# Factors and probabilities turned by TensorE, and all operations issued in the order of a list scheduling inside the kernel

## The chip, the cores and the metric

The kernel runs on one core of one Trainium2 chip. The metric is the device time of one launch in microseconds (us), the median of several runs. One core has five engines that run side by side, each taking its own instructions strictly in order: TensorE (PE: matmuls and transposes into the accumulators, PSUM), VectorE (DVE), ScalarE (ACT), GpSimd (POOL) and SyncE (SP), which here issues nearly all DMA transfers. They wait for one another through semaphores.

## The reference

One layer over 256 tokens of width 4096, in float32. A projection by `w_in` feeds 16 heads of softmax attention with a forget gate ("fox", head size 128), 32 heads of an RWKV-7 recurrence (head size 64) and a gate `z`; the gated results go through `w_out`, a residual and a LayerNorm.

```python
proj = jnp.einsum('bsd,dc->bsc', x, w_in)
...
logits = jnp.einsum('bhqd,bhkd->bhqk', qb, kf) + cb[..., :, None] - c[..., None, :]
logits = jnp.where(key_pos[None, :] <= q_pos[:, None], logits, -jnp.inf)
p = jax.nn.softmax(logits, axis=-1)
...
state = (state * w_t[:, :, None, :] + sa[..., None] * b_t[:, :, None, :]
         + v_t[..., None] * k_t[:, :, None, :])
return state, jnp.einsum('bhvk,bhk->bhv', state, r_t)
...
h = jnp.concatenate([fox_out, rwkv_out], axis=-1) * jax.nn.silu(z.astype(f32))
out = jnp.einsum('bsc,cd->bsd', h.astype(x.dtype), w_out)
x = _layernorm(ALPHA * x.astype(f32) + out.astype(f32), ln_gain, ln_bias, LN_EPS).astype(x.dtype)
```

## The kernel before

**The large matmuls.** x and every weight are split in two float32r halves, high (h) and low (l), and each product is three matmuls of 128x128 by 128x512: x high by w high (L146), x low by w high (L147), x high by w low (L148). Weights stream in pieces of 512 KB, `w{n}_{b}_{q}` (`w4_1_7` in the order, `w_7` in the profile, which leaves n and b out): SyncE loads one (L218), ScalarE makes the high half (`w_7h`, L140), VectorE the low one (`w_7l`, L141). A piece feeds 12 large matmuls. Buffers allow four raw pieces, four high and three low ones, and `weights` (L238) keeps up to three split pieces ready ahead. There are 8 head pairs n, each with 4 blocks b (block 0: r and k, 1: v of both kinds, 2 and 3: q, k and the gates of the fox heads 2n and 2n+1), each with 16 pieces q; then the output projection with 8 blocks of 16 pieces (`project`, L860 to L862). That makes 7680 large matmuls.

**The work between.** What the heads need besides runs as Python generators, which `slot` (L198) advances by a step after every two of the (j, m) steps; the order in which they emit is then the program's, apart from the framework's scheduler and from operations pinned by `keep_in_program_order` or `issue_after`. Numbers of slots to wait stand in the table `W` and in constants (LAG, LAND, BEHIND).

- `unload` takes a finished block: two VectorE transposes of `bk` (L789), a trip through HBM (`bt`) and back as `fq`, `fk`, `zf`, `zr` or `raw`. For the last pair TensorE turns them instead (`tr`, L815).
- `prepare` makes the factors `BK`, `lt` and the decays of one half of a pair (`np` on TensorE).
- `rwkv` (L505) computes a pair's recurrence by chunks of 64: the products `gp` (L517), which give `Nb` by a trip through HBM; the inverse of a triangular matrix on VectorE, 31 steps of a product and a sum (`prod`, L579, and `xc`, L582; called the solver below), whose result goes out as `td` and comes back as `T` (L589, L591); `qt` and `xp`; then for each of four chunks `rh` (L626), `up` (L653), the new state `sp` (L662, three chunks), and the read-out `yp` (L678); at last `vs`.
- Beside the solver, `turns` (L551) sends `BK`, transposed in 32x32 blocks on VectorE (L547), through HBM to get `BKt`, its full transpose, which `sp` reads; and `vt` likewise.
- `fox` (L707) is one attention head: `fsp` (L716, L717) for the logits, a softmax on VectorE and ScalarE into `lg`, the transpose of the probabilities, and `fop` (L744, L745), copied out as `fo` by ScalarE (L747). For heads 0 to 13 the probabilities are turned by VectorE in 32x32 blocks (L728) and by a trip through HBM (`turn`, L283, with four issues, and one more for `pT`, L735). For heads 14 and 15 TensorE turns them by three transposes, and ScalarE copies them out (L737 to L740).

Of the kernel before, what the change touches and what calls it, by code (L numbers as in the profile page):

```python
# [10 lines left out]
F32 = mybir.dt.float32  # L11
# [6 lines left out]
P = 128  # L18
# [63 lines left out]


@with_exitstack
def layer(ctx: ExitStack, tc: tile.TileContext, xt, xtok, w_lora, w_main, muv, w_o, up, par, mulora, fbias, lng, lnb, cst, out):
    nc = tc.nc
    PS = bass.MemoryType.PSUM
# [7 lines left out]
    def pst(name):  # L95
        return ps.tile([P, 512], F32, tag="ps", name=name)
# [27 lines left out]
    nc.vector.memset(warm, 0.0)  # L124
    tc.keep_in_program_order(nc.scalar.activation(warm, warm, AF.Tanh))
    nc.sync.dma_start(out=mul, in_=mulora)
# [17 lines left out]
    def mm(acc, at, k, hi, lo, o, n):  # L144
        tt = slice(at * P, (at + 1) * P)
        nc.tensor.matmul(acc[:, :n], xs[k][:, 0, tt], hi[:, o : o + n], start=(k == 0), stop=False)  # L146
        nc.tensor.matmul(acc[:, :n], xs[k][:, 1, tt], hi[:, o : o + n], start=False, stop=False)  # L147
        nc.tensor.matmul(acc[:, :n], xs[k][:, 0, tt], lo[:, o : o + n], start=False, stop=(k == KT - 1))  # L148

    def steps(n, last):  # L150
# [6 lines left out]
    for n, (k0, k1) in enumerate(pieces):  # L157
        for k in range(k0, k1):
            t = xpool.tile([P, 2, S], F32R, tag=f"x{k}", name=f"x{k}")
            r = x_raw[n][:, (k - k0) * S : (k - k0 + 1) * S]  # L160
            tc.keep_in_program_order(nc.scalar.copy(t[:, 0, :], r))
            nc.vector.tensor_tensor(t[:, 1, :], r, t[:, 0, :].bitcast(F32), ALU.subtract)
            xs.append(t)
        hi, lo = split(l_raw[n], (k1 - k0) * LW, f"wl{n}", spool, str(n % 3), 2 * LW)
        for j, m in steps(k1 - k0, False):
            mm(acc_l[m], m, k0 + j, hi, lo, j * LW, LW)
        hi, lo = split(w_raw[n], (k1 - k0) * OB, f"wr{n}")
        for j, m in steps(k1 - k0, k1 == KT):
            mm(acc_0[m], m, k0 + j, hi, lo, j * OB, OB)
    early.close()  # L170

# [19 lines left out]
    def wait(n):  # L191
        for _ in range(n):
            yield
# [86 lines left out]
    def issue(out, src):  # L280
        tc.keep_in_program_order(nc.sync.dma_start(out=out, in_=src))

# [112 lines left out]
    def flat(t):  # L395
        return t.rearrange("p a b -> p (a b)")
# [54 lines left out]
    def prepare(i):  # L451
# [43 lines left out]
        yield  # L495
        tc.keep_in_program_order(nc.vector.reciprocal(n2, n2))
        yield from wait(2)
# [7 lines left out]
    def rwkv(n):  # L505
# [38 lines left out]
        UV = [rp.tile([P, 2, NCH, C], F32, tag=f"UV{j}", name=f"UV{j}_{n}") for j in range(2)]  # L544
        yield from wait(W["tp"])
        for u in range(2):
            tc.keep_in_program_order(nc.vector.transpose(flat(BK[:, u]), flat(BK[:, u])))  # L547
        yield from wait(W["d1"])
        BKt = rp.tile([P, 2, NCH, P], F32, tag="shl", name=f"BKt{n}")

        def turns():  # L551
            d = yield from turn(BK.rearrange("p u c t -> p (u c) t"), f"BKt{n}", 1)
            yield from wait(2)
            issue(BKt.rearrange("p u c t -> p (u c t)"), d.rearrange("q i g a t -> (q i) (g a t)"))
            yield
            vst = UV[0].rearrange("p u c v -> p (u c v)").rearrange("p (m q) -> p m q", m=2)
            for a in range(2):
                tc.keep_in_program_order(nc.vector.transpose(vst[:, a, :], vs_[n][:, a, :]))
# [18 lines left out]
        for t, s in enumerate(range(B - 2, -1, -1)):  # L577
            w = B - 1 - s
            first = nc.vector.tensor_tensor(prod[:, :, :, s + 1 :], nb[:, :, s : s + 1, s + 1 :].to_broadcast([P, 2, NJ, w]), xc[:, :, :, s + 1 :], ALU.mult)  # L579
            if not t:  # L580
                tc.keep_in_program_order(first)
# [11 lines left out]
        vt = vs_[n].rearrange("p m (u j v) -> p m u j v", u=2, j=2)  # L593
        tc.keep_in_program_order(nc.vector.tensor_reduce(vm.rearrange("p m u j -> p (m u j)"), vs_[n].rearrange("p m (a v) -> p (m a) v", v=HD), AX.X, ALU.add))
        yield
        for j in range(2):
            o = HALF[1 - j]
            for c in range(2):
                h = HALF[c]
                for a in range(2):  # L600
                    nc.vector.scalar_tensor_tensor(
                        SV[j][o, :, 2 * a + c, :], vm[h, a, :, j].unsqueeze(2).to_broadcast([C, 2, HD]), -1.0 / HD, vt[h, a, :, j, :], ALU.mult, ALU.add
                    )
            tc.keep_in_program_order(nc.scalar.copy(UV[j][o], SV[j][o]))
            nc.gpsimd.memset(SV[j][HALF[j], :, 0, :], 0.0)
        yield from wait(W["d2"] - 1)
        for a in range(4):
            o = C * (a // 2) + B * (a % 2)
            rows = slice(B * a, B * (a + 1))
            tc.keep_in_program_order(nc.vector.transpose(X[rows].rearrange("p u c t -> p (u c) t")[:, :, o : o + B], T[rows].rearrange("p u c s -> p (u c) s")))  # L610
        qp = pst(f"qt{n}")
# [95 lines left out]
    def fox(i, q, k, vt):  # L707
# [13 lines left out]
        for m, blk in enumerate((slice(0, 1), slice(1, 3))):  # L721
# [4 lines left out]
            nc.vector.tensor_scalar(lg[:, blk, :], lg[:, blk, :], st[:, 4 + m : 5 + m], None, ALU.mult)  # L726
        if i < G - 2:
            nc.vector.transpose(flat(lg), flat(lg))  # L728
# [12 lines left out]
        yield from wait(W["fo"])  # L741
# [115 lines left out]
    def project(acc, k, j, m, hi, lo):  # L857
        hi, lo = part(hi, j), part(lo, j)
        tt = slice(m * P, (m + 1) * P)
        nc.tensor.matmul(acc, ht[k][:, 0, tt], hi, start=(k == 0), stop=False)  # L860
        nc.tensor.matmul(acc, ht[k][:, 1, tt], hi, start=False, stop=False)  # L861
        nc.tensor.matmul(acc, ht[k][:, 0, tt], lo, start=False, stop=(k == KT - 1))  # L862

    res = None
# [54 lines left out]
    for b, q in outs:  # L919
# [22 lines left out]
        if b == 0:  # L942
            while sides:
                slot()
            mid.close()
            rpool = ctx.enter_context(tc.tile_pool(name="rpool", bufs=1))
# [22 lines left out]
    def moments(m):  # L969
# [15 lines left out]
        nc.vector.tensor_copy(z[:, 0:3:2], zh.bitcast(F32).to_broadcast([P, 2]))  # L985
        last = nc.vector.tensor_tensor(z[:, 1:2], s2, zh.bitcast(F32), ALU.subtract)
        if m:
# [5 lines left out]
        rss.append(rs)  # L993
        return z, za, last.ins

# [16 lines left out]

    z0, _, last = moments(0)
    with tc.issue_after(last):
        gain(0, NB - 1)
    done_b = 0
# [10 lines left out]
    for b in range(HALVED):  # L1027
# [3 lines left out]
        wps.append(wp)  # L1031
    z1, za, last = moments(1)
    with tc.issue_after(last):
        l1 = row(z1, "1", pp, "pp")
        la = row(za, "a", pp, "pp")
        gain(1, NB - 1)
    for n in range(HALVED):
        b = HALVED + n
        finish(1, b, l1, pp, "pp")
        o = slice(n * OB, (n + 1) * OB)  # L1040
        nc.tensor.matmul(wps[n], la, rows[:, o], start=False, stop=True)
        nc.scalar.mul(res[1][:, o], wps[n], rss[1])
        store(1, b, 1)
        store(1, n, 1)


# [46 lines left out]
```

## Time and profile before

| | before |
|---|---|
| median of 3 runs | 1992.68 us (1992.07 to 1992.7) |
| span of the profiled execution | 1990.4 us, 2.3 below that median |
| PE busy | 1948.0 us |
| DVE busy | 1384.1 us |
| ACT busy | 962.3 us |
| POOL busy | 79.6 us |
| DMA | 434.03 MB, 198370 packets under 512 B |

The profile is of one execution, and every duration below comes from it; no time of that execution other than its span is given. Times are in us unless marked ns. In rows of groups stand the line, the engine, the operation, output and inputs, the count, then the busy time, the mean of one in ns, and the engine's idle time just before. A line number is that of the instruction in the kernel before; in the changed kernel all instructions are issued from one line, L311, so there groups go by the names of tiles.

### The profile page before, as it was taken

What the parts mean: (1) busy time and instruction counts of PE and PEld (TensorE: products, weight loads), DVE (VectorE), ACT (ScalarE), POOL (GpSimd) and SP (SyncE); (2) the same over time, 40 slices, a digit from 0 to 9 for tenths busy, and PEclk for the clock granted to TensorE, in tenths of its full rate; (3) what the DMA queues carried; (4) which work ended last, traced back from release to release, by engine and by line L of the source; (5) the groups of instructions that cost most, each with busy time, mean ns of one, the idle gap of its engine ahead of it and who ended that gap; (6) DMA issues with size and microseconds to landing.
All of it is one profiled execution on the core that took longest, in us unless ns stands there. A gap on an engine that the chain in (4) does not pass through costs nothing.

```text
span 1990.4 us, 28153 instructions
## 1 busy us (share of the span) xinstructions
PE 1948.0 (98%) x10063; PEld 1583.7 (80%) x10063; DVE 1384.1 (70%) x2242; ACT 962.3 (48%) x1455; POOL 79.6 (4%) x111
## 2 busy tenths in 40 slices
PE   9998999999999999999999999999999999999998
PEld 8887787788777887778777877787778878888886
DVE  6577658865886588668866886688668856755555
ACT  6552555355535554455355544554455445443333
POOL 0010001000100010001000100010001000000000
PEclk9999999999999999999999999999999999999999
DMA  9577676867786769677867786778676877866664
GB/s 335 150 230 218 196 196 214 237 205 201 224 240 202 211 212 247 201 204 213 251 200 200 219 248 198 201 221 246 197 203 210 262 281 234 259 200 200 196 190 169
DMA packets 328241, 434.03 MB, mean 218 GB/s; under 512 B 198370, under 2 KB 228852, under 8 KB 328100
## 3 DMA queue, kind: packets, MB, share of 16 engines
q1 hardware_dynamic: 327668, 431.81, 72.3%
q8 instruction: 79, 1.29, 0.3%
q14 instruction: 62, 0.51, 0.1%
q10 hardware_dynamic: 432, 0.43, 0.1%
HBM read 395.56 MB, written 36.59 MB: 217 GB/s over the span
## 4 chain that ended last, share of the span: by engine, by line
PE 85%; DVE 11%; issue 2%; ACT 1%; DMA 1%; ACTq 0%; DVEq 0%; SPq 0%
PE acc L146 20%; PE acc L148 20%; PE acc L147 19%; PE oacc L860 6%; PE oacc L861 6%; PE oacc L862 6%; DVE prod L579 3%; DVE xc L582 3%; PE yp L678 1%; PE gp L517 1%; DMA w<-in_w_main_dram 1%; PE up L653 1%; PE rh L626 1%; DVE w_7l L141 1%; DVE w_15l L141 0%
## 5 line engine op out<-in xcount | busy, mean ns | idle before, releaser
L582 DVE TENSOR_REDUCE xc<-prod 128x8 f32<-128x16 f32 (+30 forms) x248 | 72.8, 294 | 7.0
L579 DVE TENSOR_TENSOR prod<-Nb,xc 128x8 f32<-128x8 f32 (+30 forms) x248 | 72.1, 291 | 7.0
L141 DVE TENSOR_TENSOR w_0l<-w,w_0h 128x1024 fp32r<-128x1024 f32 x31 | 37.8, 1220 | 53.0 <-ACT w_0h L140 46.9
L140 ACT CAST w_0h<-w 128x1024 fp32r<-128x1024 f32 x31 | 32.6, 1053 | 74.6 <-DMA w<-in_w_main_dram 63.6
L146 PE MATMUL acc<-w_7h,x 128*128 128x512 f32 x124 | 55.8, 450 | 10.6 <-ACT w_7h L140 10.6
L141 DVE TENSOR_TENSOR w_6l<-w,w_6h 128x1024 fp32r<-128x1024 f32 x31 | 37.9, 1222 | 35.9 <-ACT w_6h L140 19.3
L148 PE MATMUL acc<-w_7l,x 128*128 128x512 f32 x124 | 54.4, 439 | 7.9 <-DVE w_7l L141 7.9
L148 PE MATMUL acc<-w_1l,x 128*128 128x512 f32 x124 | 49.1, 397 | 7.7 <-DVE w_1l L141 7.7
L141 DVE TENSOR_TENSOR w_7l<-w,w_7h 128x1024 fp32r<-128x1024 f32 x31 | 37.9, 1224 | 26.8 <-ACT w_7h L140 16.4
L898 ACT COPY bk<-acc 128x512 f32<-128x512 f32 x48 | 28.0, 586 | 57.8 <-PE acc L148 57.6
L140 ACT CAST w_5h<-w 128x1024 fp32r<-128x1024 f32 x31 | 32.6, 1051 | 46.3 <-PE acc L147 24.5
L147 PE MATMUL acc<-w_7h,x 128*128 128x512 f32 x124 | 53.8, 434 | 0.0
L141 DVE TENSOR_TENSOR w_10l<-w,w_10h 128x1024 fp32r<-128x1024 f32 x31 | 37.9, 1223 | 22.0 <-PE acc L148 18.2
L141 DVE TENSOR_TENSOR w_5l<-w,w_5h 128x1024 fp32r<-128x1024 f32 x31 | 37.9, 1222 | 22.0 <-PE acc L148 13.5
L141 DVE TENSOR_TENSOR w_12l<-w,w_12h 128x1024 fp32r<-128x1024 f32 x31 | 37.5, 1211 | 21.8 <-PE acc L148 9.0
L141 DVE TENSOR_TENSOR w_8l<-w,w_8h 128x1024 fp32r<-128x1024 f32 x31 | 37.7, 1217 | 19.6 <-ACT UV L656 13.5
L141 DVE TENSOR_TENSOR w_11l<-w,w_11h 128x1024 fp32r<-128x1024 f32 x31 | 37.9, 1221 | 19.4 <-PE acc L148 12.0
L146 PE MATMUL acc<-w_15h,x 128*128 128x512 f32 x124 | 49.8, 401 | 1.5 <-ACT w_15h L140 1.5
L146 PE MATMUL acc<-w_8h,x 128*128 128x512 f32 x124 | 50.3, 406 | 0.8 <-ACT w_8h L140 0.8
L146 PE MATMUL acc<-w_9h,x 128*128 128x512 f32 x124 | 49.0, 395 | 1.6 <-ACT w_9h L140 1.6
L146 PE MATMUL acc<-w_5h,x 128*128 128x512 f32 x124 | 50.6, 408 | 0.0
L148 PE MATMUL acc<-w_5l,x 128*128 128x512 f32 x124 | 48.3, 398 | 2.1 <-DVE w_5l L141 2.1
(811 smaller groups left out, 6479.7 us busy)
## 6 DMA issues: line engine op xcount, KB each, us to landing
w<-in_w_main_dram SPq DMA_DIRECT2D x496, 512.0 KB
wo<-in_w_o_dram SPq DMA_DIRECT2D x128, 512.0 KB
bt<-bk SPq DMA_DIRECT2D x88, 128.0 KB
Nb<-nd SPq DMA_DIRECT2D x16, 512.0 KB
wr<-in_w_main_dram SPq DMA_DIRECT2D x15, 512.0 KB
hd<-hl SPq DMA_DIRECT2D x29, 256.0 KB
h<-hd SPq DMA_DIRECT2D x29, 256.0 KB
raw<-bt SPq DMA_DIRECT2D x16, 256.0 KB
```

The source lines that it names most:

```text
L140: nc.scalar.copy(hi[:, :n], src[:, :n])
L141: nc.vector.tensor_tensor(lo[:, :n], src[:, :n], hi[:, :n].bitcast(F32), ALU.subtract)
L146: nc.tensor.matmul(acc[:, :n], xs[k][:, 0, tt], hi[:, o : o + n], start=(k == 0), stop=False)
L147: nc.tensor.matmul(acc[:, :n], xs[k][:, 1, tt], hi[:, o : o + n], start=False, stop=False)
L148: nc.tensor.matmul(acc[:, :n], xs[k][:, 0, tt], lo[:, o : o + n], start=False, stop=(k == KT - 1))
L517: nc.tensor.matmul(gp[u][j][:, c * P : (c + 1) * P], BK[h, u, c, :], lt[j][h, u, c, :], start=True, stop=True)
L579: first = nc.vector.tensor_tensor(prod[:, :, :, s + 1 :], nb[:, :, s : s + 1, s + 1 :].to_broadcast([P, 2, NJ, w]), xc[:, :, :, s + 1 :], ...
L582: nc.vector.tensor_reduce(xc[:, :, :, s : s + 1], prod[:, :, :, s:], AX.X, ALU.add)
L860: nc.tensor.matmul(acc, ht[k][:, 0, tt], hi, start=(k == 0), stop=False)
L861: nc.tensor.matmul(acc, ht[k][:, 1, tt], hi, start=False, stop=False)
L862: nc.tensor.matmul(acc, ht[k][:, 0, tt], lo, start=False, stop=(k == KT - 1))
L898: nc.scalar.copy(bk[:, m, :], acc[m])
```

## The change

**Turns.** `BKt` is now made by three TensorE transposes for each half of a pair (`bkt`, 48 in all) and a copy by ScalarE. The probabilities of heads 0 to 13 are made as those of 14 and 15 were (`fpt`, 42 more). The 16 VectorE transposes of `BK`, the 14 of `lg`, and the DMA issues of both trips (110) go.

**Order.** `nc` is now an object that notes every operation with its operands instead of issuing it. `flush` (after the first block, after the first output block, and at the end) then issues all in an order found by a list scheduling: a clock for each engine; an estimate, `span_of`, of how long an operation holds its engine and when its result can be seen; dependencies by the bounding boxes (`extent`) of what it touches in a tile; buffers of the pools as a resource (`places`). At each step the engine that can start first takes, of the operations that are ready by then, the one written first (`key`); loads and splits of weights count as written 60 operations earlier (`AHEAD`). A change between large matmuls (`main`) and others costs 100 ns on TensorE (`SWITCH`). All operations are pinned in that order, on all engines; the single pins and `issue_after` go.

```diff
+def extent(ap):
...
+    p0, f0 = divmod(int(ap.offset), f)
+    p1, f1 = p0 + 1, f0 + 1
+    for a, n in dims:
+        if a >= f and a % f == 0:
+            p1 += (n - 1) * (a // f)
+        else:
+            f1 += (n - 1) * abs(a)
+    return p0, p1, f0, f1
+
...
+def span_of(engine, name, args, out, ins):
...
+    if engine == "tensor":
+        rhs = ins[-1] if name == "matmul" else ins[0]
+        n = columns(out)
+        if name == "transpose":
...
+        return cost, cost + 205
+    if engine == "sync":
+        n = columns(out) if out.space != bass.MemoryType.DRAM else columns(ins[0])
+        size = 4 * min(run(out), run(ins[0]), 1024)
+        total = 4 * 128 * n
+        return (620 if size <= 128 else 390), (total / size / 16 * (8 + size / 27), 2000)
+    n = max(columns(a) for a in [out, *ins])
...
+    def take(self, engine, call, name, args, kwargs):
...
+        op.hold, op.lag = span_of(engine, name, kwargs, outs[0], ins)
+        op.after, op.touches = set(), []
+        op.main = self.main
+        op.key = self.count - self.sooner
...
+        for ap, writing in [(a, False) for a in ins] + [(a, True) for a in outs]:
...
+            for other, box in self.writes[where] + (self.reads[where] if writing else []):
+                if box[0] < at[1] and at[0] < box[1] and box[2] < at[3] and at[2] < box[3] and other is not op:
+                    op.after.add(other)
+            (self.writes if writing else self.reads)[where].append((op, at))
+        self.ops.append(op)
...
+    def flush(self, stay=()):
...
+        while len(made) < len(ops):
+            best = None
+            for e in ENGINES:
...
+                if ready[e]:
+                    at = self.free[e]
+                elif soon[e]:
+                    at = max(self.free[e], soon[e][0][0])
+                else:
+                    continue
+                if best is None or at < best[0]:
+                    best = at, e
...
+            at, e = best
+            while soon[e] and soon[e][0][0] <= at:
+                _, _, _, op = heapq.heappop(soon[e])
+                heapq.heappush(ready[e], (op.key, id(op), op))
+            _, _, op = heapq.heappop(ready[e])
+            wait = self.places(op)
...
+            if wait > at:
+                op.ready = wait
+                heapq.heappush(soon[e], (wait, op.key, id(op), op))
+                continue
...
+        made.sort(key=lambda o: o.start)
+        for op in made:
+            ins = op.call(*op.args, **op.kwargs)
+            self.tc.keep_in_program_order(ins)
+            op.call = op.args = op.kwargs = None
+            op.after = ()
+        return made
...
+    def begin(self, op, at):
+        if op.engine == "tensor":
+            if op.main != self.kind:
+                at += SWITCH
+                self.kind = op.main
+        op.start = at
+        self.free[op.engine] = at + op.hold
+        if op.engine == "sync":
+            size, lag = op.lag
+            self.moved = max(self.moved, at + op.hold) + size
+            op.end = max(self.moved, at + op.hold) + lag - 400
+        else:
+            op.end = at + op.lag
+
+
...
-    nc = tc.nc
+    nc = Later(tc)
...
     def mm(acc, at, k, hi, lo, o, n):
+        nc.main = True
         nc.tensor.matmul(acc[:, :n], xs[k][:, 0, tt], hi[:, o : o + n], start=(k == 0), stop=False)
         nc.tensor.matmul(acc[:, :n], xs[k][:, 1, tt], hi[:, o : o + n], start=False, stop=False)
         nc.tensor.matmul(acc[:, :n], xs[k][:, 0, tt], lo[:, o : o + n], start=False, stop=(k == KT - 1))
+        nc.main = False
...
     def weights(name):
+        nc.sooner = AHEAD
         while len(ready) < 3 and (stream or raws):
             fetch()
+        nc.sooner = 0
         got, hi, lo = ready.pop(0)
         assert got == name
         return hi, lo
...
+        BKt = rp.tile([P, 2, NCH - 1, P], F32, tag="shl", name=f"BKt{n}")
         for u in range(2):
-            tc.keep_in_program_order(nc.vector.transpose(flat(BK[:, u]), flat(BK[:, u])))
+            bt = pst(f"bkt{n}_{u}")
+            for c in range(NCH - 1):
+                nc.tensor.transpose(bt[:, c * P : (c + 1) * P], BK[:, u, c, :], ident)
+            nc.scalar.copy(flat(BKt[:, u]), bt[:, : (NCH - 1) * P])
         yield from wait(W["d1"])
-        BKt = rp.tile([P, 2, NCH, P], F32, tag="shl", name=f"BKt{n}")
...
         def turns():
-            d = yield from turn(BK.rearrange("p u c t -> p (u c) t"), f"BKt{n}", 1)
-            yield from wait(2)
-            issue(BKt.rearrange("p u c t -> p (u c t)"), d.rearrange("q i g a t -> (q i) (g a t)"))
-            yield
...
-        if i < G - 2:
-            nc.vector.transpose(flat(lg), flat(lg))
         yield from wait(W["fp"])
-        if i < G - 2:
-            ld = yield from turn(lg, f"fpt{i}")
-            yield
         pT = rp.tile([P, 3 * P], F32, tag="nb", name=f"pT{i}")
-        if i < G - 2:
-            issue(pT, ld.rearrange("q i m a t -> (q i) (m a t)"))
-        else:
-            pt = pst(f"fpt{i}")
-            for m in range(3):
-                nc.tensor.transpose(pt[:, m * P : (m + 1) * P], lg[:, m, :], ident)
-            nc.scalar.copy(pT, pt[:, : 3 * P])
+        pt = pst(f"fpt{i}")
+        for m in range(3):
+            nc.tensor.transpose(pt[:, m * P : (m + 1) * P], lg[:, m, :], ident)
+        nc.scalar.copy(pT, pt[:, : 3 * P])
         yield from wait(W["fo"])
         op = pst(f"fop{i}")
...
```

Where it moves instructions: three places of pair 4, whose heads are 8 and 9, and in whose block 1 the previous pair's head 7 ends. First TensorE around the output of head 7, before: `fop7` stands between the two last matmuls of a step of `w4_1_6`.

```order
L146 MATMUL acc4_1_1_8089<-w4_1_6h_8192,x12_437 128x512
L147 MATMUL acc4_1_1_8089<-w4_1_6h_8192,x12_437 128x512
L148 MATMUL acc4_1_1_8089<-w4_1_6l_8193,x12_437 128x512
L146 MATMUL acc4_1_0_8088<-w4_1_6h_8192,x13_440 128x512
L147 MATMUL acc4_1_0_8088<-w4_1_6h_8192,x13_440 128x512
L744 MATMUL fop7_8202<-pT7_8166,vt3_6718 128x256
L745 MATMUL fop7_8202<-pT7_8166,vt3_6718 128x128
L148 MATMUL acc4_1_0_8088<-w4_1_6l_8193,x13_440 128x512
```

The same in the changed kernel, the three transposes `fpt7` included; "x2" are two alike in a row.

```order
L311 MATMUL fpt7_2208<-cs_72,lg7_2181 128x128 x3
...
L311 MATMUL acc4_1_0_2194<-w4_1_2h_2197,x5_154 128x512 x2
L311 MATMUL acc4_1_0_2194<-w4_1_2l_2198,x5_154 128x512
L311 MATMUL acc4_1_1_2195<-w4_1_2h_2197,x5_154 128x512 x2
L311 MATMUL acc4_1_1_2195<-w4_1_2l_2198,x5_154 128x512
L311 MATMUL fop7_2213<-pT7_2207,vt3_1955 128x256
L311 MATMUL fop7_2213<-pT7_2207,vt3_1955 128x128
L311 MATMUL acc4_1_0_2194<-w4_1_3h_2205,x6_159 128x512 x2
L311 MATMUL acc4_1_0_2194<-w4_1_3l_2206,x6_159 128x512
```

`fop7` and `fo7` behind it have moved up by more than three pieces of weights, and the turn of the probabilities stands on TensorE 18 large matmuls ahead of it. Among the even heads `fsp8` moves the other way, from `w4_3_8` to `w4_3_11`, and `fop8` stands three large matmuls behind the last of `fpt8`.

Second VectorE in the solver of pair 4, before, from the split `w4_3_0l` to the split `w4_3_1l` (the rows left out are two more `prod` and an `xc`).

```order
L141 TENSOR_TENSOR w4_3_0l_8856<-w4_3_0_8807,w4_3_0h_8855 128x1024
L579 TENSOR_TENSOR prod4_8773<-Nb4_8639,xc4_8774 128x8x18
L582 TENSOR_REDUCE xc4_8774<-prod4_8773 128x8
...
L789 STREAM_TRANSPOSE bk4_2_8901<-bk4_2_8901 128x512
L582 TENSOR_REDUCE xc4_8774<-prod4_8773 128x8
L579 TENSOR_TENSOR prod4_8773<-Nb4_8639,xc4_8774 128x8x21
L789 STREAM_TRANSPOSE bk4_2_8901<-bk4_2_8901 128x512
L582 TENSOR_REDUCE xc4_8774<-prod4_8773 128x8
L579 TENSOR_TENSOR prod4_8773<-Nb4_8639,xc4_8774 128x8x22
L141 TENSOR_TENSOR w4_3_1l_8880<-w4_3_1_8830,w4_3_1h_8879 128x1024
```

In the changed kernel, the same two splits:

```order
L311 TENSOR_TENSOR w4_3_0l_2353<-w4_3_0_2344,w4_3_0h_2352 128x1024
L311 TENSOR_REDUCE xc4_2340<-prod4_2339 128x8
L311 TENSOR_TENSOR prod4_2339<-Nb4_2313,xc4_2340 128x8x15
L311 TENSOR_REDUCE xc4_2340<-prod4_2339 128x8
L311 TENSOR_TENSOR prod4_2339<-Nb4_2313,xc4_2340 128x8x16
L311 TENSOR_REDUCE xc4_2340<-prod4_2339 128x8
L311 TENSOR_TENSOR w4_3_1l_2356<-w4_3_1_2348,w4_3_1h_2355 128x1024
L311 TENSOR_TENSOR prod4_2339<-Nb4_2313,xc4_2340 128x8x17
L311 TENSOR_REDUCE xc4_2340<-prod4_2339 128x8
L311 TENSOR_TENSOR prod4_2339<-Nb4_2313,xc4_2340 128x8x18
L311 STREAM_TRANSPOSE bk4_2_2358<-bk4_2_2358 128x512
```

The 11 operations between the two splits have become five, and the turn of `bk4_2` comes after the second split.

Third TensorE at the state and the read-out of chunk 1 of pair 4 (`sp4_1` and `yp4`; the large matmuls are the next pair's), before:

```order
L148 MATMUL acc5_0_1_9337<-w5_0_4l_9427,x8_361 128x512
L662 MATMUL sp4_1_9510<-UV1_4_8661,BKt4_8772 64x64 x2
L662 MATMUL sp4_1_9510<-UV0_4_8660,BKt4_8772 64x64 x2
L678 MATMUL yp4_9436<-lt1_4_8247,SV1_4_8659 64x64
L678 MATMUL yp4_9436<-lt0_4_8246,SV0_4_8658 64x64
L678 MATMUL yp4_9436<-gb1_839,UV1_4_8661 64x64
L678 MATMUL yp4_9436<-gb0_838,UV0_4_8660 64x64
L678 MATMUL yp4_9436<-lt1_4_8247,SV1_4_8659 64x64
L678 MATMUL yp4_9436<-lt0_4_8246,SV0_4_8658 64x64
```

In the changed kernel:

```order
L311 MATMUL acc5_0_1_2431<-w5_0_4l_2445,x8_165 128x512
L311 MATMUL sp4_1_2459<-UV1_4_2317,BKt4_2324 64x64 x2
L311 MATMUL sp4_1_2459<-UV0_4_2316,BKt4_2324 64x64 x2
L311 MATMUL yp4_2446<-lt1_4_2233,SV1_4_2315 64x64
L311 MATMUL yp4_2446<-lt0_4_2232,SV0_4_2314 64x64
L311 MATMUL yp4_2446<-gb1_830,UV1_4_2317 64x64
L311 MATMUL yp4_2446<-gb0_829,UV0_4_2316 64x64
L311 MATMUL acc5_0_0_2430<-w5_0_4h_2444,x9_166 128x512
L311 MATMUL yp4_2446<-lt1_4_2233,SV1_4_2315 64x64
L311 MATMUL yp4_2446<-gb1_830,UV1_4_2317 64x64
```

The eight matmuls of `yp4` for this chunk, in one run before, are now cut by a large matmul after the first four. Counted over the whole order, runs of small matmuls between large ones were 216 and are 268.

More of the change, by code (lines that the diff above doesn't have):

```diff
@@ L1 @@
+import bisect
+import heapq
 import math
@@ L81, in constants @@
     return cst
+ENGINES = ("tensor", "vector", "scalar", "gpsimd", "sync")
+AHEAD = 60
+SWITCH = 100
+def extent(ap):
+    t = ap.tensor
+    shape = [int(n) for n in t.shape]
+    f = 1
+    for n in shape[1:]:
+        f *= n
+    dims = [(int(a), int(n)) for a, n in ap.ap if int(n) > 1]
+    if ap.space == bass.MemoryType.DRAM:
+        return 0, 1, int(ap.offset), int(ap.offset) + sum((n - 1) * abs(a) for a, n in dims) + 1
+    p0, f0 = divmod(int(ap.offset), f)
[6 more added lines that the diff above has]
+    return p0, p1, f0, f1
@@ L944, in layer @@
                 slot()
+            nc.flush([t for _, *hl in ready for t in hl] + [raw for _, raw in raws])
             mid.close()
@@ L1011, in finish @@
         nc.vector.scalar_tensor_tensor(res[m][:, o], res[m][:, o], rss[m], wp, ALU.mult, ALU.add)
-    z0, _, last = moments(0)
-    with tc.issue_after(last):
-        gain(0, NB - 1)
+    z0, _ = moments(0)
+    gain(0, NB - 1)
     done_b = 0
@@ L1031, in layer @@
         wps.append(wp)
[L1032 to L1036, printed above, removed]
+    z1, za = moments(1)
+    l1 = row(z1, "1", pp, "pp")
+    la = row(za, "a", pp, "pp")
+    gain(1, NB - 1)
     for n in range(HALVED):
```

187 lines of the change are left out of this document (174 added, 13 removed).

## The prediction

> **What bounds the kernel now.** I read the page first. The second row quoted here gives each engine's busy time with its share of the span, the third the chain that ended last.
>
> ```profile
> span 1990.4 us, 28153 instructions
> PE 1948.0 (98%) x10063; PEld 1583.7 (80%) x10063; DVE 1384.1 (70%) x2242; ACT 962.3 (48%) x1455; POOL 79.6 (4%) x111
> PE 85%; DVE 11%; issue 2%; ACT 1%; DMA 1%; ACTq 0%; DVEq 0%; SPq 0%
> ```
>
> TensorE is the bound: it works 98% of the span and the chain is its own for 85%. So a change can gain only where TensorE stands or runs slowly, and every matmul that it adds is paid in full. Next I read what TensorE waited for: total, number of waits, longest.
>
> ```profile
> PE acc L146 <- ACT w_7h L140: 10.6, 7, 2.3
> PE acc L148 <- DVE w_7l L141: 7.9, 8, 4.2
> PE acc L148 <- DVE w_1l L141: 7.7, 8, 1.5
> PE acc L148 <- DVE w_5l L141: 2.1, 7, 0.8
> PE acc L146 <- ACT w_9h L140: 1.6, 1, 1.6
> PE acc L146 <- ACT w_15h L140: 1.5, 1, 1.5
> ```
>
> These six rows, the longest, are 31.4 us in 32 waits, all for a split weight (w..h from ScalarE, w..l from VectorE), most of them once in each head pair. The timeline of TensorE through one of them (start, duration, engine, line, idle before) shows that a wait costs more than its idle time.
>
> ```profile
> 893.06 0.39 PE L148 MATMUL acc<-w_6l,x 128*128 128x512 f32 x1
> 894.83 0.50 PE L146 MATMUL acc<-w_7h,x 128*128 128x512 f32 x1 [1.38 <-ACT w_7h L140]
> 895.16 0.40 PE L147 MATMUL acc<-w_7h,x 128*128 128x512 f32 x1
> 896.09 0.50 PE L148 MATMUL acc<-w_7l,x 128*128 128x512 f32 x1 [0.53 <-DVE w_7l L141]
> 896.42 0.52 PE L146 MATMUL acc<-w_7h,x 128*128 128x512 f32 x1
> 896.74 0.63 PE L147 MATMUL acc<-w_7h,x 128*128 128x512 f32 x1
> ...
> 900.07 0.39 PE L146 MATMUL acc<-w_8h,x 128*128 128x512 f32 x1
> 900.30 0.40 PE L147 MATMUL acc<-w_8h,x 128*128 128x512 f32 x1
> ```
>
> Undisturbed, one large matmul starts 0.23 us after another (900.07 to 900.30). Over the first wait it is 1.77 us, so 0.16 more than idle time and pitch, and the next start comes 0.10 late (0.33 for 0.23). Then the clock was halved: from 896.42 to 900.07 nine matmuls take 3.65 us in place of 9 x 0.23 = 2.07, a loss of 1.6. The stretches of the trace show the granted clock there (eighth column: PEclk).
>
> ```profile
> 180.00:206.00 26.00, 19.16 (x71) 14.41 (x70) 19.62 (x40) 8.29 (x15) 0.00 (x0) 0.87 0.52 161
> 888.00:900.00 12.00, 10.10 (x38) 7.61 (x37) 6.04 (x11) 6.35 (x10) 0.11 (x1) 0.86 0.60 199
> ```
>
> So 14% of 12 us, 3.4 us at half clock, belong to one such halt; the first pair's, at 190, is twice as long. The Trainium skill, page "TensorE: Matmul & The Clock Gate", section "Part 1: The HAM clock gate", lets the clock fall after at least one idle window of about 3.4 us. The row disagrees in part: here it fell after idle times of 1.38 and 0.53 us, with matmuls between.
>
> Who made w_7h late? ScalarE's rows before it:
>
> ```profile
> 892.56 0.37 ACT L747 COPY fo<-fop 128x256 f32<-128x256 f32 x1 [9.79 <-PE fop L745]
> ...
> 893.74 1.04 ACT L140 CAST w_7h<-w 128x1024 fp32r<-128x1024 f32 x1
> ```
>
> ScalarE stood 9.8 us with w_7h queued behind the attention output fo, whose matmul waited for probabilities that went through HBM to be turned. The w_1l waits are VectorE's: the order in the section on the change shows 11 operations of the solver (nine prod and xc, two turns of bk) between w4_3_0l and w4_3_1l.
>
> **Part by part: the waits.** The probabilities now reach fop by three transposes and a copy, and in the new order fop7 stands at w4_1_3 instead of in w4_1_6, so fo is done before w_7h is due; the DMA that kept ScalarE is gone. On VectorE the splits come every four to six solver operations. The first pair's longest halt (4.2, for w_7l) is the solver's too, and is cut up likewise. I let all six rows go: 31.4 idle, 32 times 0.26 (8.3), and the half clock: seven times 1.6, and about 2 more for the first pair's longer stretch (13): 53 us.
>
> **The turns on TensorE.** 48 transposes for the factors and 42 for the probabilities are added. Before has this operation for the last pair:
>
> ```profile
> 1568.90 0.60 PE L815 MATMUL tr<-cs,bk 128*128 128x128 f32 x4
> 1569.26 0.48 PE L146 MATMUL acc<-w_1h,x 128*128 128x512 f32 x1
> 1569.58 0.40 PE L147 MATMUL acc<-w_1h,x 128*128 128x512 f32 x1
> ```
>
> Four push the next large matmul by 0.36 and the one after by 0.09: 0.11 each, 90 of them 9.9 us, all on the path. What they replace costs the path nothing: 30 VectorE transposes, whose rows follow, and 110 DMA issues. VectorE's 18 us fell inside its 30% idle time except where the waits above have counted it; ScalarE gets 30 copies instead, each shorter than a split (1.04 in the row above), so under 31 us on an engine busy 48%. If that cover went, splits would be late again: the first rival.
>
> ```profile
> L547 DVE STREAM_TRANSPOSE BK<-BK 128x512 f32<-128x512 f32 x16 | 10.3, 680 | 0.0
> L728 DVE STREAM_TRANSPOSE lg<-lg 128x384 f32<-128x384 f32 x14 | 7.9, 567 | 0.2
> ```
>
> The Trainium skill, same page, section "Part 4: PE-mode transpose", puts a transpose at about 275 ns in a kernel's context; by it the 90 would be 24.8 us. The rows agree with it as a latency only; the cost of a fourth one in a row is 0.11.
>
> **The read-outs in two.** The new order breaks the yp matmuls of a chunk in two runs, with one or five large matmuls between. Runs of small matmuls between large ones number 216 before and 268 now, counted in the order: 8 for the factors, 21 for probabilities, 25 for yp, less two merged. What a run costs beside its matmuls:
>
> ```profile
> 829.42 0.29 PE L678 MATMUL yp<-gb,UV 128*64 128x64 f32 x4
> 829.54 0.29 PE L678 MATMUL yp<-lt,SV 128*64 128x64 f32 x4
> ...
> 831.14 0.40 PE L148 MATMUL acc<-w_3l,x 128*128 128x512 f32 x1
> 831.47 0.45 PE L626 MATMUL rh<-SV,lt 128*64 128x64 f32 x8
> 831.86 0.50 PE L146 MATMUL acc<-w_3h,x 128*128 128x512 f32 x1
> 832.19 0.40 PE L147 MATMUL acc<-w_3h,x 128*128 128x512 f32 x1
> ```
>
> Eight records of rh take 0.10 late start, 0.39, and 0.10 late after: 0.59. Four records in a row are 0.12 apart, so eight are 0.23, and the run itself 0.36. 25 more: 9.0 us; two merged: -0.7. Whether one large matmul is enough to pay the full price between two runs no row shows; bounds 0.2 and 0.36, so 5 to 9. I take 9.0.
>
> **New waits.** The fixed order puts small matmuls where their inputs are reckoned to be just ready, and TensorE takes them in turn; behind one that waits, all large matmuls queue. I see two places. Even heads: fsp8 stands at w4_3_11 instead of w4_3_8, behind a longer chain through SyncE (solver, td, T, and only then fq8). The planner reckons 1.6 us from a transfer's end to its landing, plus 0.39 for the issue. SyncE's rows:
>
> ```profile
> 799.20 0.90 SPq L589 DMA_DIRECT2D td<-xc  x2
> ...
> 803.41 3.64 SPq L591 DMA_DIRECT2D T<-td  x8
> ```
>
> From the second td (799.65) to the T that waited for it are 3.8 us; the planner's sum, a load ahead of it included, is nearer 3. Two such hops make fsp8 about 1 us late (0 to 1.5). With 0.26 that is 1.3 us, eight times 10. VectorE and SyncE are held up as long, but splits are up to two buffers ahead. Odd heads: a table load now stands directly before their exponential, which the planner does not price:
>
> ```profile
> L367 ACT ACT_TABLE_LOAD x7 | 9.0, 1283 | 0.1
> ```
>
> 30 large matmuls (6.9 us) lie between fsp7 and fpt7, so I take a quarter of 1.28 seven times, 2 us (bounds 0 and 9). New waits: 12 us, bounds 0 and 25 (below nothing is excluded: what goes has been counted whole).
>
> **The sum.** 1990.4 - 53 + 9.9 + 9.0 - 0.7 + 12 = 1967.6 us of span. The median of the three runs, 1992.68, is 2.3 above this execution's span; so 1970 us. A measurement of this kernel tells about 0.2% (4 us) from no change.
>
> **Rivals.**
> - *New waits large enough to halve the clock* (0.15): at the eight even heads 1.5 us each, and 1.6 of half clock behind: 8 x 3.4 = 27 in place of 10: 1987. For it: the two DMA hops. Against: the w_1l waits, 0.96 us each in the mean by the row above, left the clock whole, as the stretch below shows, in which one of them falls. By the clock rule of the Trainium skill cited above the clock would hold through 1.5 us too, and this case would be 8 x 1.76 = 14: 1974.
>
> ```profile
> 768.00:780.00 12.00, 11.04 (x49) 8.80 (x48) 11.48 (x27) 5.52 (x7) 0.00 (x0) 1.00 0.74 200
> ```
>
> - *VectorE stays late* (0.07): only ScalarE's halt goes; w_1l, w_5l and the first pair keep 7.7 + 2.1 idle and 15 x 0.26, and the first pair about half of its halts, some 5: 19 more, 1989. Against: the solver is cut up in the order.
> - *Transposes do not overlap* (0.03): each costs its latency. A row of tr lasts 0.60 for four started over 0.33, so one lasts 0.27; 90 x 0.27 = 24, 14 more: 1984. The rule on transposes cited above from the Trainium skill would be this case.
> - *Slower* (0.09): TensorE now turns the probabilities itself, so a head whose softmax is late stops TensorE and not only ScalarE. If all 16 heads stop it as w_7 did (1.38 + 0.53 + 0.52 + 1.6 = 4.0), that is 64 in place of 12: 2022. It decides from 34.8 us of new waits on (53 - 18.2), 2.2 us per head. For it: fop8 stands three large matmuls behind fpt8. Against: fsp to fpt leaves 13 to 30 matmuls.
>
> **Numbers.** My case has 0.66. Its own bounds are 1954 (no new wait, and yp at the lower price) to 1983 (25 of new waits); the first and third rival lie at 1987 and 1984, so 0.84 lie between 1955 and 1988. Faster by over 0.2%: 0.66 + 0.15 + 0.03, less 0.01 for a tail, and half of the second rival: 0.87; within 0.2%, its other half and a little: 0.04; slower: 0.09.
>
> **What would show it.** Right: the w_7h and w_1l rows gone from TensorE's waits, no stretch below full clock between 10 and 1900 us, 0.11 per transpose, 0.36 per extra run, waits at fsp of even heads near 1 us. Wrong: waits of splits still there, half clock behind fsp or fpt, TensorE's small matmuls waiting over 35 us in all.

## The result and the profile after

The changed kernel takes 2006.83 us (median of 4 runs, 2003.66 to 2012.1), the kernel before 1992.38 beside it: a ratio of 1.008, 95% interval 1.0057 to 1.0103. It is slower by 0.8%, where 1970 us and a range up to 1988 had been forecast. The profiled execution spans 2005.7 us, 15.3 more than that of before.

The page of the changed kernel, its span, the engines, and the chain that ended last:

```profile
span 2005.7 us, 28250 instructions
PE 1960.6 (98%) x10153; PEld 1589.4 (79%) x10153; DVE 1384.5 (69%) x2212; ACT 982.8 (49%) x1485; POOL 84.5 (4%) x111
PE 80%; DVE 11%; DMA 6%; issue 2%; ACT 1%; SPq 0%; POOL 0%; ACTq 0%; DVEq 0%; POOLq 0%
```

TensorE is the bound as before, but 6% of the chain are now DMA, where it was 1%. What TensorE waited for (total, times, longest):

```profile
PE acc L311 <- ACT w_0h L311: 9.4, 1, 9.4
PE fpt L311 <- DVE lg L311: 7.5, 13, 0.8
PE np L311 <- DVE shl L311: 3.9, 14, 0.7
PE oacc L311 <- ACT bk L311: 2.9, 1, 2.9
PE accl L311 <- ACT x L311: 2.7, 1, 2.7
PE bkt L311 <- DVE lt L311: 2.7, 7, 0.8
PE fsp L311 <- ACT fq L311: 1.9, 3, 0.9
PE acc L311 <- ACT bk L311: 1.8, 1, 1.8
```

All six rows of before, waits for split weights, are gone. In their place stand two kinds of waits: single long ones at the begin (`accl`, `w_0h`), in the first pair (`acc` for `bk`) and at the output projection (`oacc`), and 37 short ones at small matmuls (`fpt`, `np`, `bkt`, `fsp`). The first of the following stretches answers to that of before in which w_7 had halved the clock (PEclk eighth), and the second is a whole steady pair with several short waits; both show the full clock. The last three show where the clock was halved in the changed kernel: behind the waits for w_0h, for `bk` in the first pair, and of `oacc`.

```profile
902.00:914.00 12.00, 12.00 (x55) 9.94 (x54) 6.02 (x5) 4.99 (x5) 1.41 (x2) 1.00 0.92 281
992.00:1190.00 198.00, 195.85 (x1048) 158.26 (x1047) 144.53 (x241) 101.52 (x157) 9.40 (x12) 1.00 0.74 208
70.00:90.00 20.00, 10.55 (x48) 8.04 (x47) 4.14 (x5) 5.70 (x11) 3.36 (x7) 0.74 0.51 163
180.00:206.00 26.00, 24.01 (x98) 19.05 (x97) 22.90 (x58) 11.00 (x14) 0.00 (x0) 0.93 0.86 229
1620.00:1634.00 14.00, 11.10 (x109) 8.48 (x108) 6.04 (x7) 7.08 (x13) 0.00 (x0) 0.88 1.01 378
```

Setting the start of the same large matmul in both traces side by side tells where the time went. After the first block (large matmul 192) the changed kernel is 13.6 us behind; at the first matmul of the output projection (6144) 8.2; a block later (6336) 14.8, and so to the end. So nearly eight pairs of steady work gave back only 5.4 us, and the two edges cost 20.

**The first block.** SyncE's queue before, then in the changed kernel, at the end of the first block:

```profile
48.21 20.72 SPq L218 DMA_DIRECT2D w<-in_w_main_dram  x6
```

```profile
75.75 0.57 SPq L311 DMA_DIRECT2D vd<-zero  x2
...
77.59 2.06 SPq L311 DMA_DIRECT2D w<-in_w_main_dram  x4
```

Before, six loads of the next weights leave from 48 us on. Now all of them stand behind `vd<-zero`. That tile and its neighbours lie in memory that the pool of the first block gives back; GpSimd's rows show how long that takes:

```profile
72.75 0.96 POOL L311 MEMSET X<- 128x1024 f32 x1 [71.49 <-PE accl L311]
...
75.42 0.30 POOL L311 MEMSET zero<- 1x256 f32 x1
```

GpSimd stands 71.5 us for the last reader of the old pool, as it stood 67.4 us in the kernel before, where no weight load was behind it. The list scheduling does not know of that memory: for it, `zero` is ready at once and written first, so `vd<-zero` comes first in SyncE's queue, and the weights, which need nothing, wait behind it.

**The output projection.** ScalarE's rows at its begin, and the wait on TensorE:

```profile
1624.80 1.04 ACT L311 CAST wo_2h<-wo 128x1024 fp32r<-128x1024 f32 x1 [1.59 <-DMA wo<-in_w_o_dram]
1625.75 0.58 ACT L311 COPY bk<-acc 128x512 f32<-128x512 f32 x1
```

```profile
1626.38 0.72 PE L311 MATMUL oacc<-wo_0h,h 128*128 128x512 f32 x2 [2.90 <-ACT bk L311]
```

The copy that `oacc` waits for stands on ScalarE behind the split of a weight that has not landed.

### The profile page after: what moved, and what is told of

Same layout as the page of the kernel before. It is cut to its first block, busy times and chain, and to the rows that moved or that the text cites. A ratio compares the mean times of both kernels' runs of the same rounds, so it can differ in the third digit from the quotient of the medians.

```text
span 2005.7 us, 28250 instructions
## 1 busy us (share of the span) xinstructions
PE 1960.6 (98%) x10153; PEld 1589.4 (79%) x10153; DVE 1384.5 (69%) x2212; ACT 982.8 (49%) x1485; POOL 84.5 (4%) x111
## 4 chain that ended last, share of the span: by engine, by line
PE 80%; DVE 11%; DMA 6%; issue 2%; ACT 1%; SPq 0%; POOL 0%; ACTq 0%; DVEq 0%; POOLq 0%
PE acc L311 56%; PE oacc L311 16%; DMA Nb<-nd 1%; DMA w<-in_w_main_dram 1%; DVE prod L311 1%; PE accl L311 1%; DMA wo<-in_w_o_dram 1%; DVE xc L311 1%; DVE lt L311 1%; PE yp L311 1%; PE gp L311 1%; DVE w_13l L311 1%; PE up L311 1%; PE rh L311 1%; DVE w_14l L311 1%
## 5 line engine op out<-in xcount | busy, mean ns | idle before, releaser
L311 PE MATMUL acc<-w_0h,x 128*128 128x512 f32 x248 | 80.2, 402 | 11.5 <-ACT w_0h L311 9.4
L311 PE MATMUL acc<-w_4h,x 128*128 128x512 f32 x248 | 79.5, 398 | 0.0
L311 PE MATMUL acc<-w_11h,x 128*128 128x512 f32 x248 | 79.1, 396 | 0.0
L311 PE MATMUL acc<-w_3h,x 128*128 128x512 f32 x248 | 78.5, 398 | 0.0
L311 PE MATMUL acc<-w_1h,x 128*128 128x512 f32 x248 | 78.5, 397 | 0.0
L311 PE MATMUL acc<-w_2h,x 128*128 128x512 f32 x248 | 78.2, 395 | 0.0
L311 PE MATMUL acc<-w_6h,x 128*128 128x512 f32 x248 | 78.1, 396 | 0.0
L311 PE MATMUL acc<-w_13h,x 128*128 128x512 f32 x248 | 77.5, 392 | 0.0
L311 PE MATMUL acc<-w_12h,x 128*128 128x512 f32 x248 | 77.4, 393 | 0.0
L311 PE MATMUL acc<-w_10h,x 128*128 128x512 f32 x248 | 76.6, 390 | 0.0
```

What stands on the lines that cost most here:

```text
L311: ins = op.call(*op.args, **op.kwargs)
```

## The experiments

**The two parts of the change apart.** First the kernel before with the turns alone:

```diff
-            tc.keep_in_program_order(nc.vector.transpose(flat(BK[:, u]), flat(BK[:, u])))
+            bt = pst(f"bkt{n}_{u}")
+            for c in range(NCH - 1):
+                nc.tensor.transpose(bt[:, c * P : (c + 1) * P], BK[:, u, c, :], ident)
+            nc.scalar.copy(flat(BKt[:, u]), bt[:, : (NCH - 1) * P])
...
-        if i < G - 2:
-            ld = yield from turn(lg, f"fpt{i}")
```

> The kernel before with the 90 transposes on TensorE, and its own order (no list scheduling). If the transposes cost 0.11 us each and end ScalarE's halt before w_7h, the seven half-clock halts (3.6 us each) and part of the first pair's go and 10 us come: about 1972 us, 1 per cent under before. If the fixed order was needed for that, because a late softmax now stops TensorE itself in the old slots, it stays at 1990 us or above.

1955.12 us; ratio 0.9819 (0.9804 to 0.9834). The turns alone are a gain of 37 us, 17 more than expected. TensorE's waits for split weights:

```profile
PE acc L148 <- DVE w_7l L141: 5.8, 1, 5.8
...
PE acc L146 <- ACT w_8h L140: 0.9, 1, 0.9
```

Not only w_7h and w_7l of the steady pairs are gone: w_1l and w_5l are, too. Only the first pair's halt is left. The transposes wait for nothing (in the steady pairs 30 large matmuls lie between `fsp` and `fpt` of a head), and cost little:

```profile
980.52 0.39 PE L148 MATMUL acc<-w_10l,x 128*128 128x512 f32 x1
980.75 0.27 PE L730 MATMUL fpt<-cs,lg 128*128 128x128 f32 x1
980.77 0.48 PE L146 MATMUL acc<-w_11h,x 128*128 128x512 f32 x1
981.09 0.39 PE L147 MATMUL acc<-w_11h,x 128*128 128x512 f32 x1
981.33 0.38 PE L730 MATMUL fpt<-cs,lg 128*128 128x128 f32 x2
981.46 0.48 PE L148 MATMUL acc<-w_11l,x 128*128 128x512 f32 x1
```

One transpose between two large matmuls makes them start 0.25 us apart for 0.23, two 0.37; the start after that comes 0.09 late as well (980.77 to 981.09 is 0.32). Timed again:

> The same kernel as turns_only, timed again beside the next one: 1955 us. If that value was the chip's and not the kernel's, it moves by more than 4 us.

1956.4 us, ratio 0.9823 (0.9809 to 0.9836): it is repeated within 1.3 us. Next, the probabilities alone:

```diff
-            ld = yield from turn(lg, f"fpt{i}")
...
-            issue(pT, ld.rearrange("q i m a t -> (q i) (m a t)"))
+        nc.scalar.copy(pT, pt[:, : 3 * P])
```

> The kernel before, in its own order, with only the probabilities turned by TensorE (42 transposes), BKt still made by VectorE and through HBM. If the w_7h and w_7l halts came from ScalarE standing before fo, they all go and the w_1l and w_5l rows stay: 1962 to 1967 us. If the freed VectorE time and SyncE issues of BKt were half of the gain, 1973 us or above.

1969.01 us; ratio 0.9893 (0.9869 to 0.9917), some 21 us: a little less than expected.

```profile
PE acc L148 <- DVE w_1l L141: 8.1, 7, 1.7
PE acc L148 <- DVE w_7l L141: 4.2, 1, 4.2
PE acc L148 <- DVE w_5l L141: 2.1, 7, 0.8
```

So the halt at w_7 was ScalarE's before `fo`, as the prediction had it. The rows of w_1l and w_5l stay; they go with the turn of `BKt`, for another 14 us (17 if each kernel is set against the runs of before beside it). VectorE's order shows how: in turns_only the split `w4_3_1l` stands six solver operations behind `w4_3_0l` and ahead of both turns of `bk`, where before and fpt_only have eleven operations with both turns. Transposes, DMA issues and steps of a generator went out together with `BKt`; which of them moved the split, no run shows. Last, the list scheduling without the turns: the edits of `BKt` and of the probabilities are undone, the rest is as in the changed kernel. Here and in all kernels below, operations whose keys tie stand in the order of writing; no kernel has that rule alone, so what it does is part of each value.

> The changed kernel with both turns back on VectorE and through HBM, so the list scheduling alone. The turns alone gave 37.5 us. If the two parts of the change add up, this kernel is 37 us above the changed one: 2044 us. If the list order by itself ends the halts that the turns ended (it places fop after the DMA that it reckons with, so ScalarE does not stand before w_7h), the turns have nothing left to gain under it: within 8 us of the changed kernel, 1999 to 2015 us, with no w_7h row among TensorE's waits.

2033.09 us; ratio 1.0215 (1.019 to 1.024). Neither case: the turns gain under the list order as well, but 26 us and not 37. There is no w_7h row, but others:

```profile
PE fop L311 <- DMA pT<-fpt: 14.3, 7, 3.0
PE acc L311 <- ACT w_0h L311: 9.1, 1, 9.1
PE gp L311 <- DVE BK L311: 8.1, 7, 2.3
```

The order put `fop` where its model had the probabilities landed; they came up to 3 us later, and now TensorE itself stands. The four kernels together:

| | old order | list order |
|---|---|---|
| turns on VectorE and through HBM | 1992.4 us | 2033.1 us |
| turns on TensorE | 1955.1 us | 2006.8 us |

The list order costs 41 us without the turns and 52 with them. The four come from three comparisons, beside which the kernel before took 1989.8 to 1992.7 us, so such differences are good to some 3 us.

**What the list order costs, piece by piece.** Three corrections, each in the changed kernel without the other two (the kernel that the expectations call calib has all three). The first (start):

```diff
     if engine == "scalar":
+        if name == "dma_start":
+            return 460, 2500
...
+        self.base = max(o.end for o in made)
...
-self.slots.setdefault(tag, [[0.0] * (t.tag_meta.bufs or 1), []])
+self.slots.setdefault(tag, [[self.base] * (t.tag_meta.bufs or 1), []])
```

> The changed kernel, whose list scheduling is told two things: that a DMA issued by ScalarE lands after 2.5 us and not 0.4, and that tiles of a pool opened after a flush are free only when all operations of that flush have ended. If the 13.6 us that it is behind after the first block come from the first loads and from weight loads queued on SyncE behind DMAs that wait for the freed memory, the first large matmul starts at 5.7 us again, the 9.4 us wait for w_0h goes, and the time is 1993 to 1995 us. If they come from the HBM or from the barrier itself, the time stays at 2004 to 2007 us.

1992.1 us, equal to before (ratio 1.0003, 0.9989 to 1.0017); as the first case had it. The loads leave as early as in the kernel before:

```profile
48.12 20.72 SPq L315 DMA_DIRECT2D w<-in_w_main_dram  x6
```

The first large matmul starts at 5.6 us in place of 8.4, and after two blocks the kernel is 15.8 us ahead of the changed one. The smaller part is the price of three loads on ScalarE's queue: reckoned as a copy of 0.4 us, they put the splits of later pieces ahead of the first copy of x. The second (exact):

```diff
-                if box[0] < at[1] and at[0] < box[1] and box[2] < at[3] and at[2] < box[3] and other is not op:
+                if (meet(box, at) or writing and is_psum(ap) and other.engine == engine == "tensor") and other is not op:
```

`meet` compares lists of column ranges, and matmuls into one accumulator tile keep their order.

> The changed kernel with exact regions in place of bounding boxes in the list scheduling, so that the eight read-out matmuls of both halves stand in one run again: 24 runs of small matmuls fewer. If a run costs 0.36 us beside its matmuls whatever stands between, 8.6 us less than the changed kernel: 1998 us. If one large matmul between two runs is not enough to pay the price, 5 us less or nothing: 2002 us or above.

2000.47 us; ratio 1.0043 (1.0026 to 1.006), 6.4 us less: between the two cases. A chunk's read-out in two runs in the changed kernel:

```profile
1040.20 0.29 PE L311 MATMUL yp<-lt,SV 128*64 128x64 f32 x4
1040.32 0.29 PE L311 MATMUL yp<-gb,UV 128*64 128x64 f32 x4
1040.54 0.73 PE L311 MATMUL acc<-w_3h,x 128*128 128x512 f32 x2
1041.11 0.40 PE L311 MATMUL acc<-w_3l,x 128*128 128x512 f32 x1
1041.34 0.63 PE L311 MATMUL acc<-w_3h,x 128*128 128x512 f32 x2
1041.90 0.34 PE L311 MATMUL yp<-lt,SV 128*64 128x64 f32 x4
1042.06 0.29 PE L311 MATMUL yp<-gb,UV 128*64 128x64 f32 x4
```

The trace of a steady pair gives 0.36 us for each cut, so 8.6 in all; in the total, 1.7 us of that are given back by a first large matmul that started later in this run (10.15 us for 8.42). The third, first as slack for the small matmuls (again with the order in one accumulator kept):

```diff
-        return o.end
+        return o.end + (800 if op.engine == "tensor" and not op.main else 0)
```

> The changed kernel with 0.8 us added to the time at which the list scheduling lets TensorE's small matmuls see what another engine made (matmuls into one accumulator bank keep their order, too). If the new waits at np, bkt, fpt and fsp come from durations reckoned too short, their 16 us of idle time go, with what hangs on it about 20 us: 1987 us. If small matmuls come late for another reason (DMA landings, buffers), the waits stay or turn into waits for splits: 2000 us or above.

2004.5 us; ratio 1.0064 (1.0046 to 1.0082): hardly a gain. `fsp` moves back as well as `fpt`, so that of the 0.8 us only two large matmuls (0.45 us) come to the softmax between them, and the `fpt` row is what it was (7.7 in 14). It also cuts the read-outs anew: runs of small matmuls number 7 more than in the changed kernel. Waiting longer everywhere was the wrong cure. Then as prices nearer to the trace, with that order kept, too:

```diff
-            t = 60 + 6.6 * n
+            t = 190 + 6.6 * n
...
-        return t - 80, t + 35
+        return t - 80, t + 120
...
-        return t - 95, t + 35
+        return t - 95, t + 120
...
-        return cost, cost + 205
+        return cost, cost + 400
```

> The changed kernel with only the third correction of calib: the prices nearer to the trace. If the waits at np, bkt, fpt and fsp come from prices too low, most of their 16.0 us of idle time goes, with slower starts about 20 us: 1987 us. If they go only together with the other two corrections, above 1998 us, and the fpt row stays near 7.5 us.

1989.05 us; ratio 0.9986 (0.9976 to 0.9995), 18 us less than the changed kernel. The rows:

```profile
PE acc L311 <- ACT w_0h L311: 9.0, 1, 9.0
...
PE bkt L311 <- DVE lt L311: 2.1, 5, 0.5
PE np L311 <- DVE shl L311: 1.9, 7, 0.7
...
PE fpt L311 <- DVE lg L311: 0.8, 1, 0.8
```

From 16.0 us in 37 waits, 6.2 in 15 are left (`fsp` 1.4 in 2), and the edge at w_0h stays, as it should. Runs of small matmuls are 11 fewer as well, some 4 us at 0.36 each. One old price could not be right: a reciprocal of one column held VectorE for -13 ns. The operation taken next then got a start 13 ns earlier and was sorted ahead of it, and so a split of 1.2 us could come into the middle of a softmax. VectorE's rows in the changed kernel, and the two waits that follow on TensorE:

```profile
1016.42 1.22 DVE L311 TENSOR_TENSOR w_14l<-w,w_14h 128x1024 fp32r<-128x1024 f32 x1
1017.55 0.16 DVE L311 RECIPROCAL fst<-fst 128x1 f32<-128x1 f32 x1
1017.74 0.29 DVE L311 TENSOR_SCALAR lg<-lg,fst 128x128 f32<-128x128 f32 x1
```

```profile
1018.17 0.30 PE L311 MATMUL fpt<-cs,lg 128*128 128x128 f32 x1 [0.69 <-DVE lg L311]
1018.23 0.48 PE L311 MATMUL acc<-w_12l,x 128*128 128x512 f32 x1
1019.13 0.44 PE L311 MATMUL fpt<-cs,lg 128*128 128x128 f32 x2 [0.42 <-DVE lg L311]
```

Which of the four prices matters most was not tried, so that the reciprocal's is the main one is not shown. Then the corrections together, two and three of them:

> The changed kernel with the first two corrections of calib (start and exact) and the old prices. If the corrections add up, 14.7 and 6.3 us less than the changed kernel: 1986 us, with the fpt row near 7.5 us. If calib's gain is mostly one mechanism that each shows in part, 1972 us or less.

1985.22 us; ratio 0.9974 (0.9958 to 0.9989): they add up (21.6 for 14.7 and 6.4).

> The changed kernel with a better-informed list scheduling: the two corrections of the kernel called start, the exact regions of the kernel called exact, and prices nearer to the trace (a reciprocal of one column 0.13 us longer, every result of VectorE and ScalarE seen 0.085 us later, a small matmul's 0.195 us later). If the list order loses only by what its model has wrong, start gives 14.7, exact 6.3, and the waits at np, bkt, fpt and fsp (about 20 us) go: 1962 to 1968 us, still not under the 1955 us of the turns in the old order. If the waits only move, about 1985 us.

1960.65 us; ratio 0.985 (0.9819 to 0.988). All three give 46 us of the 52 that the list order costs. The first pair is even 6 us shorter than with the turns in the old order; 8 are lost in the steady pairs and 4 in the output projection, 2.6 of them in its first block, so it stays behind the 1955 of the turns alone. That last loss I tried to mend with a lower bandwidth in the prices:

```diff
-(total / size / 16 * (8 + size / 27), 2000)
+(total / size / 16 * (8 + size / 22), 2000)
```

> The kernel called calib with one price more: a transfer's bandwidth reckoned some 20 per cent lower, so that in the order of ScalarE the copies of the last block stand ahead of the split of the third output weight, which waits for its load. If the 4.3 us that calib loses to turns_only at the begin of the output projection are this, 1956 us, the same as turns_only, with a shorter first pair and a longer steady part. If the weights are simply later there, 1960 us as before.

1975.81 us; ratio 0.9918 (0.9905 to 0.9932): neither case, 15 us worse than calib. The output projection did gain 3 us, but the factors of each pair now come later in the order, and their first consumer on TensorE stands for them in six pairs (the row of waits, one such place, and its stretch):

```profile
PE gp L329 <- DVE BK L329: 9.7, 6, 2.1
```

```profile
1123.35 1.73 PE L329 MATMUL gp<-lt,BK 64*128 64x128 f32 x16 [2.12 <-DVE BK L329]
```

```profile
1115.00:1130.00 15.00, 12.76 (x70) 10.20 (x69) 13.54 (x17) 4.08 (x6) 4.82 (x3) 0.89 0.61 177
```

One price changed at one place made the order 15 us dearer elsewhere. It also halved the clock for a while: 0.89 over 15 us, so 3.3 us at half clock, here and behind three more of these waits.

## Why the prediction was wrong

The direction failed, by its list of terms and not by its reading of the kernel before.

- **Waits that go (-53): right in place and about in size.** All six rows went. Between large matmuls 192 and 6144, what large matmuls lose to waits and half clock (the time beyond 0.227 us from start to start, runs of small matmuls left aside) fell by 49 us, and by 51 without the 2.0 at half clock behind w_0h. But the prediction gave the new order the credit for VectorE's part. The kernels apart show that the turns alone remove both: w_7 with the probabilities, w_1l and w_5l with `BKt`. The prediction held that what the transposes replace costs the path nothing, since VectorE's share "fell inside its 30% idle time except where the waits above have counted it"; with `BKt` turned on TensorE the w_1l and w_5l waits went without any list order.
- **Transposes (+9.9): right.** In turns_only six in a run cost 0.57 us and three 0.25, and the 0.09 by which the start after is late: 8 x 0.66 and 14 x 0.34 make 10. The rival in which they do not overlap (24 us) is out. The Trainium skill, page "TensorE: Matmul & The Clock Gate", section "Part 4: PE-mode transpose", has about 275 ns for one; the trace has that as the duration of a record (272 and 273 ns), but not as the price of one among matmuls.
- **Read-outs in two (+9.0): about right.** 0.36 each in a steady pair as taken, 6.4 in the total.
- **New waits (+12): half of what came.** 16.0 us in 37 waits, with 0.26 each for the slower starts 25.6; set against the same runs of small matmuls without waits in turns_only, they cost 25.5. The places were wrong, too: `fsp`, on which the term rested, has 1.9 us in 3; `fpt`, mostly of the even heads, `np` and `bkt` have the rest. In the list order only 13 to 16 large matmuls lie between `fsp` and `fpt` of an even head (30 in turns_only). I compared the DMA prices of the list scheduling with the trace, and not those of the short VectorE operations, where the model was off.
- **The edges (0): missed.** This is the step that turned the sign: "The fixed order puts small matmuls where their inputs are reckoned to be just ready" was weighed in the steady pairs alone; the first block and the begin of the output have no term in its sum, and no reason is given for that. The first block costs 13.6 and then 2.0 at half clock. The begin of the output costs 6.5, among them the 2.9 of `oacc` and 1.7 of half clock behind it.

The sum with what was measured: -51 + 10 + 7.5 (the read-outs ahead of the output) + 25.5 + 15.6 + 6.5 = 14, against 15.3 in the spans. The rest is not assigned.

The prediction's sign "no stretch below full clock between 10 and 1900 us" failed as well, but by the three long waits shown above. The rival that ended slower named late softmaxes that halve the clock, from 34.8 us of new waits on. The place was partly right (`fpt`), the mechanism not: in the changed kernel no short wait halved the clock, and the new waits came to 25.5. Without the first block's edge the change would have been no slower than before, as start shows.

## What to carry to other kernels

Time the parts of a change apart before trusting their sum: here one part gained 37 us and the other lost 52. A fixed order for all engines is as good as its model at the worst place. Check first where the model cannot know something (here memory that a pool gives back at a flush, and the queue behind it: 14.7 us together with the price of ScalarE's loads), then its prices (18 us for four of them; one, a reciprocal reckoned at -13 ns, let a split of 1.2 us into a softmax). On SyncE's queue, which issues in order, `vd<-zero` waited at the head to 75.75 us and held the weight loads behind it to 77.59, which needed nothing and had left at 48.21 before.

## What the runs showed of the hardware

- In the changed kernel TensorE's clock stayed full through 37 waits of up to 0.9 us, and was halved behind single ones of 9.4, 1.85 and 2.9. The length of a wait alone does not decide: the same wait of 1.85 us left the clock whole in the kernel slack (PEclk 1.00 from 180 to 192 us), one of 1.53 halved it in fpt_only (0.86 from 1580 to 1592), and one of 2.37 did not in order_only (1.00 from 685 to 695). What else decides, these runs do not show. The Trainium skill, page "TensorE: Matmul & The Clock Gate", section "Part 1: The HAM clock gate", asks for an idle window of about 3.4 us; the falls behind 1.53, 1.85 and 2.9 disagree in the size, though not in kind.
- A wait of 0.26 us before the second half of a run of six transposes made the run 0.45 us dearer than the same six without it (1.02 for 0.57 beyond the pitch). Over all 37 waits it was 25.5 us for 16.0 of idle time: a short wait costs some 1.6 times its idle time.
